# The down projection with every block sum on VectorE, its seven products in another order, and the last six k pairs summed token tile by token tile

## The chip, the cores and the metric

The kernel runs on one core of a Trainium2 chip. The engines that matter here are TensorE (PE in the profile, its weight loads PEld), VectorE (DVE), ScalarE (ACT) and GpSimd (POOL); SyncE (SP) issues most DMAs. Each engine takes its instructions in the order in which they stand, so an instruction that waits holds back all behind it. The metric is the device time of one execution in microseconds (us), median over the runs.

## The reference, cut to what matters

One decoder layer on 1024 tokens of width 1024: a token mixer, a cross-attention and a gated MLP, each between two RMSNorms. The change touches the last product of the MLP and the last norm with its residual:

```
u = causal_dwconv(h @ w_up, conv_w) + conv_b
a, b = split(u, 2)
y = (silu(a) * b) @ w_down            # (1024 x 2816) @ (2816 x 1024)
out = h2 + y * rsqrt(mean(y * y) + EPS) * g[5]
```

All of it is float32, with the accuracy of float32 products.

## The kernel before

**Where the stage lies.** The up projection runs column tile by column tile (Strassen's scheme, `strassen_pair`). Its last call ends with two short convolutions (`conv3`, L1127), a SiLU and a gate product (L1133) on VectorE and ScalarE; `silu(a) * b` goes to DRAM as `mid_d`, 22 rows of 128 channels x 1024 tokens. Then the down projection begins; TensorE passes from one to the other without a barrier.

**Strassen's scheme for the down projection.** The tokens are cut into two halves, the output columns into two halves, and the 22 k tiles into even and odd ones, which gives 11 k pairs (`kp`) and, for each pair, blocks A11 to A22 of the activations and B11 to B22 of the weights, all 128x512. `PRODS` lists the seven products M1 to M7; each is a sum of one or two A blocks times a sum of one or two B blocks, added up in PSUM over the 11 pairs. A product takes four PSUM banks, one for each tile of 128 tokens.

**A step** is one k pair of one product, so there are 7 x 11 = 77. `down_operands` makes its operands: it loads the blocks (an A block once, `a_block`; the B blocks each time into `rb`), sums them, and splits each sum into a high part, rounded to the matmul format (ScalarE, L132 or L1312 or L1308), and a low part, what the rounding lost (VectorE, L133 or L1313 or L1309). `mm3` then issues high x high, high x low and low x high (L236, L237, L238) for each of the four token tiles: twelve matmuls of 512 columns a step. Operands are made four steps ahead (`fetch(4)`, the tag `w` has four buffers).

**Who sums.** M4 and M3 have a sum of B blocks: GpSimd (L1301). M5 and M2 have a sum of A blocks: GpSimd (L1299). M1, M6 and M7 have both: A on GpSimd (L1299), B on VectorE (L1301). M2's B block is negated in its split.

**After a product** `done` adds its banks into the accumulators `yacc` (ScalarE copies for M4 and M3, VectorE adds, L1322, for the rest). When a half row of `yacc` is complete, `square` (ScalarE, L1318) sums its squares and `gained` multiplies it by the norm's gain (VectorE, L1326). `final` works out the norm's factor (L1338, L213 to L217), applies it with the residual `fin` (VectorE, L1332, two halves) and stores. `fin` has two buffers; `residual` (L1343) loads one. M6 and M7 add onto the banks of M2 and M1. The last four k pairs of M7 are walked token tile by token tile, so that the tiles end one after another; the residual of a tile is asked for just before its matmuls.

A scheduler sorts the instructions of each engine; the order inside one engine is not quite that of the code.

Of the kernel before, what the change touches and what calls it, by code (L numbers as in the profile page):

```python
# [1475 lines left out]
```

## Time and profile before

| | us |
|---|---|
| median of 3 runs (1509.54 to 1512.87) | 1512.68 |
| the profiled execution | 1516.54 |
| its span, first to last instruction | 1514.5 |
| TensorE busy in the span | 1445.2 (95%) |
| VectorE busy | 1179.0 (78%) |
| ScalarE busy | 698.9 (46%) |
| GpSimd busy | 301.2 (20%) |

The first matmul of the down projection starts at 1263.0 us of the span, the last at 1496.8. A busy share is a mean over the whole program; what holds in this stage is read from rows of this stage. Times in rows are us from the start of the span; the profile calls every product bank `M`, every operand `wM`, every block sum `sM`, every A block `ma`, every loaded B pair `rbM`.

### The profile page before, as it was taken

How to read it: one execution, taken by the hardware profiler on the slowest of the kernel's cores; microseconds unless marked ns; L12 is line 12 of the kernel's file. 1: busy time of each engine (PE TensorE's matmuls, PEld its weight loads, DVE VectorE, ACT ScalarE, POOL GpSimd, SP SyncE). 2: the span in 40 equal slices, each digit the busy share in tenths (PEclk: the TensorE clock that was granted, in tenths of full speed). 3: DMA queues.
4: the chain of work that ended last, by engine and by line, in shares of the span. 5: the costliest groups of instructions: out<-in, count | busy, mean ns of one | idle time of the engine just before them, and what ended most of it. 6: DMA issues, size and time to landing. Idle time of an engine off the chain costs nothing.

```text
span 1514.5 us, 19535 instructions
## 1 busy us (share of the span) xinstructions
PE 1445.2 (95%) x7099; PEld 1189.5 (79%) x7099; DVE 1179.0 (78%) x1938; ACT 698.9 (46%) x1348; POOL 301.2 (20%) x195
## 2 busy tenths in 40 slices
PE   6999999999999899999999979999999999999984
PEld 6878888888897778788888858888888887887763
DVE  6799999983577777734555877888888888869996
ACT  6527455533565445433433534444444444554342
POOL 0000000000000000000001543333333334655651
PEclk9999999999999999999999989999999999999997
DMA  7523133339656765401423112222222227964545
GB/s 250 173 75 124 44 112 84 112 111 327 185 160 211 241 209 179 149 1 42 154 85 110 43 56 84 78 76 84 84 84 84 84 84 260 317 201 161 184 160 176
DMA packets 118560, 205.74 MB, mean 136 GB/s; under 512 B 17184, under 2 KB 58816, under 8 KB 118464
## 3 DMA queue, kind: packets, MB, share of 16 engines
q1 hardware_dynamic: 95488, 155.99, 33.2%
q10 hardware_dynamic: 22976, 48.51, 8.6%
q8 instruction: 56, 0.92, 0.3%
q14 instruction: 40, 0.33, 0.1%
HBM read 153.58 MB, written 50.87 MB: 135 GB/s over the span
## 4 chain that ended last, share of the span: by engine, by line
PE 70%; DVE 13%; DMA 8%; issue 4%; ACT 3%; POOL 1%; SPq 0%; DVEq 0%; ACTq 0%; POOLq 0%
PE st L236 8%; PE st L238 8%; PE st L237 8%; PE pj L238 6%; PE pj L236 6%; PE pj L237 6%; DVE wM L133 3%; PE M L237 2%; PE M L236 2%; PE M L238 2%; PE y L237 2%; PE y L238 2%; PE y L236 2%; PE sc L237 1%; PE sc L236 1%
## 5 line engine op out<-in xcount | busy, mean ns | idle before, releaser
L352 DVE SCALAR_TENSOR_TENSOR ca<-sg,par,ca 128x1023 f32<-128x1023 f32 (+18 forms) x120 | 150.3, 1268 | 1.1
L236 PE MATMUL pj<-xT,w_in 128*128 128x512 f32 x384 | 150.8, 393 | 0.1
L238 PE MATMUL pj<-xT,w_in 128*128 128x512 f32 x384 | 150.3, 391 | 0.5 <-DVE w_in L133 0.5
L237 PE MATMUL pj<-xT,w_in 128*128 128x512 f32 x384 | 149.9, 390 | 0.0
L1198 POOL TENSOR_TENSOR xr<-x,x 128x256 f32<-128x256 f32 x32 | 32.4, 1045 | 582.6 <-DVE hr L1106 565.4
L237 PE MATMUL M<-wM 128*128 128x512 f32 x308 | 124.9, 406 | 9.8 <-DVE wM L133 5.7
L1127 DVE SCALAR_TENSOR_TENSOR ua<-ua,par 128x1023 f32<-128x1023 f32 x88 | 117.0, 1329 | 11.3 <-ACT ua L1125 8.4
L236 PE MATMUL M<-wM 128*128 128x512 f32 x308 | 120.8, 397 | 2.2 <-ACT wM L132 2.2
L238 PE MATMUL M<-wM 128*128 128x512 f32 x308 | 121.6, 395 | 0.0
L236 PE MATMUL st<-xT,wst 128*128 128x512 f32 x304 | 118.7, 391 | 0.0
L238 PE MATMUL st<-xT,wst 128*128 128x512 f32 x304 | 118.4, 390 | 0.0
L237 PE MATMUL st<-xT,wst 128*128 128x512 f32 x304 | 118.2, 389 | 0.0
L1299 POOL TENSOR_TENSOR sM<-ma,ma 128x512 f32<-128x512 f32 x55 | 95.1, 1732 | 73.5 <-DVE wM L133 45.0
L236 PE MATMUL st<-x,wst 128*128 128x512 f32 x228 | 93.3, 409 | 9.6 <-ACT ua L1216 5.7
L238 PE MATMUL st<-x,wst 128*128 128x512 f32 x228 | 91.0, 399 | 0.0
L237 PE MATMUL st<-x,wst 128*128 128x512 f32 x228 | 90.9, 399 | 0.0
L1157 DVE TENSOR_TENSOR wst<-sums,wst 128x512 fp32r<-128x512 f32 x76 | 60.7, 819 | 35.0 <-ACT wst L1156 35.0
L1156 ACT ACTIVATE wst<-sums 128x512 fp32r<-128x512 f32 x76 | 43.8, 621 | 90.0 <-POOL sums L1151 90.0
L237 PEld LDWEIGHTS M<-wM 128*128 128x128 f32 x308 | 58.9, 191 | 33.0 <-DVE wM L133 15.3
L238 PEld LDWEIGHTS pj<-xT,w_in 128*128 128x128 f32 x384 | 72.1, 188 | 15.4 <-DVE w_in L133 0.8
L236 PEld LDWEIGHTS pj<-xT,w_in 128*128 128x128 f32 x384 | 72.0, 188 | 14.9 <-ACT w_in L132 0.3
L237 PEld LDWEIGHTS pj<-xT,w_in 128*128 128x128 f32 x384 | 72.2, 188 | 14.5
(380 smaller groups left out, 3782.6 us busy)
## 6 DMA issues: line engine op xcount, KB each, us to landing
rbM<-in_w_down SPq DMA_DIRECT2D x132, 256.0 KB, 3.5
raw_up<-in_w_up SPq DMA_DIRECT2D x44, 512.0 KB, 3.6
raw_in<-in_w_in SPq DMA_DIRECT2D x24, 512.0 KB, 3.7
mid_d<-ua ACTq DMA_DIRECT2D x22, 512.0 KB, 2.6
ma<-mid_d SPq DMA_DIRECT2D x44, 256.0 KB, 5.0
raw_kv<-in_w_kv SPq DMA_DIRECT2D x16, 512.0 KB, 4.2
h_d<-h ACTq DMA_DIRECT2D x16, 512.0 KB, 2.7
xr<-in_x ACTq DMA_DIRECT2D x8, 512.0 KB, 5.3
```

The lines of the kernel that those rows point to most:

```text
L133: dve.tensor_tensor(w[:, 1], raw, w[:, 0], op=ALU.subtract)
L236: pe.matmul(o, lhsT=wh, rhs=xh, start=start, stop=False, skip_group_check=onto)
L237: pe.matmul(o, lhsT=wh, rhs=xl, start=False, stop=False, skip_group_check=onto)
L238: pe.matmul(o, lhsT=wl, rhs=xh, start=False, stop=stop, skip_group_check=onto)
L352: dve.scalar_tensor_tensor(out=ca[:, d:], in0=sg[:, :T - d], scalar=par[:, wb + 30 - d:wb + 31 - d], in1=ca[:, d:], op0=ALU.mult, op1=ALU.add)
L1127: dve.scalar_tensor_tensor(out=a[:, d:], in0=u[:, :T - d], scalar=fw(2 - d), in1=a[:, d:], op0=ALU.mult, op1=ALU.add)
L1156: act.activation(w[:, i, 0], op[s], AF.Copy)
L1157: dve.tensor_tensor(w[:, i, 1], op[s], w[:, i, 0], op=ALU.subtract)
L1198: nc.gpsimd.tensor_tensor(raw[n], X[n][0][:, :, s], X[n][1][:, :, s], op=ALU.add)
L1299: nc.gpsimd.tensor_tensor(sums[:, 0], A_s[0], A_s[1], op=alu(ab[2]))
```

## The change

In the down projection GpSimd computes nothing any more. Sums of B blocks (L1305) and of A blocks (L1312) are done by VectorE in place, in the tile `rb` itself, so the tag `sum` goes. Signs are placed otherwise, so that every A sum is a difference and M2 needs no negation. The B tiles have six buffers in place of four (`raw` 2, `braw` 4). The A21 blocks lie in three tiles of four.

The products run M4, M3, M2, M1, M6, M5, M7 (before: M4, M3, M5, M2, M1, M6, M7). M5 now starts on the banks that M6 has just ended. `gained` moves from `done` to the list `pend`, which is now worked off at odd k pairs of every product.

The last six k pairs of M7 (before: four) are walked token tile by token tile. Three of them (5, 6, 7) have operands in the A21 tiles, free by then, and are made among the last steps of M5. All four residuals are asked for before that walk; two of them lie in `raw` tiles.

```diff
-    LAST = 4
+    LAST = 6
+    PRODS = (("M4", 0, ("22",), ("21", "11")), ("M3", 1, ("11",), ("12", "22")),
+             ("M2", 0, ("22", "21"), ("11",)), ("M1", 1, ("11", "22"), ("11", "22")),
+             ("M6", 0, ("21", "11"), ("11", "12")), ("M5", 0, ("11", "12"), ("22",)),
+             ("M7", 1, ("12", "22"), ("21", "22")))
+    ENDP = len(PRODS) - 1
+    EXTRA = (5, 6, 7)
...
-        name, ab, bb = PRODS[m]
-        p, tag = ((wpool, "raw"), (dr, "braw"))[n_step[0] % 2]
+        name, _, ab, bb = PRODS[m]
+        p, tag, bufs = (wpool, "raw", 2) if n_step[0] % 3 == 0 else (dr, "braw", 4)
...
-        w = wpool.tile([P, 2, 2, 512], F32R, tag="w", name=f"w{name}_{kp}", bufs=4)
-        if len(ab) == 3 or len(bb) == 3:
-            sums = dr.tile([P, 2, 512], F32, tag="sum", name=f"s{name}_{kp}", bufs=2)
-        if len(ab) == 3:
-            nc.gpsimd.tensor_tensor(sums[:, 0], A_s[0], A_s[1], op=alu(ab[2]))
-        if len(bb) == 3:
-            (dve if len(ab) == 3 else nc.gpsimd).tensor_tensor(sums[:, 1], rb[:, 0], rb[:, 1], op=alu(bb[2]))
...
+        sync.dma_start(out=rb[:, 1], in_=at(bb[0]))
+        if len(bb) == 2:
+            sync.dma_start(out=rb[:, 0], in_=at(bb[1]))
+            dve.tensor_tensor(rb[:, 1], rb[:, 1], rb[:, 0], op=ALU.subtract if name == "M1" else ALU.add)
+        if m == ENDP and kp in EXTRA:
+            w = dl.tile([P, 2, 2, 512], F32R, tag="a21", name=f"w{name}_{kp}", bufs=3)
         else:
+            w = wpool.tile([P, 2, 2, 512], F32R, tag="w", name=f"w{name}_{kp}", bufs=4)
+        if len(ab) == 2:
+            dve.tensor_tensor(rb[:, 0], A_s[0], A_s[1], op=ALU.subtract)
+            split(w, rb)
+        else:
+            for i, r in enumerate((A_s[0], rb[:, 1])):
+                act.activation(w[:, 0, i], r, AF.Copy)
+                dve.tensor_tensor(w[:, 1, i], r, w[:, 0, i], op=ALU.subtract)
...
+        fin = raw_tile((P, D), f"fin{t}") if last else dl.tile([P, D], F32, tag="fin", name=f"fin{t}", bufs=2)
...
-            gained(hi, 1)
-            pend.append(lambda: final(hi, residual(hi), 0))
+            pend.append(lambda: (gained(hi, 1), final(hi, residual(hi), 0)))
+        elif name == "M5":
+            add_to(lo, 0, o)
+            add_to(lo, 1, o, -1)
+            square(lo, 1)
+            pend.append(lambda: gained(lo, 1))
...
+    todo = [(m, kp) for m in range(ENDP) for kp in range(NP)]
+    for n, kp in enumerate(EXTRA):
+        todo.insert(len(todo) - 3 + n, (ENDP, kp))
+    todo += [(ENDP, kp) for kp in range(NP) if kp not in EXTRA]
...
-            if pend and name == "M7" and kp % 2:
+            if pend and kp % 2 and kp < NP - 1:
...
-    fetch(LAST)
+    fetch()
+    fins.update({q: residual(q, q > 1) for q in range(4)})
     for q in range(4):
-        fins[q] = residual(q)
         for kp in range(NP - LAST, NP):
```

The order of the instructions shows three places. The first is VectorE at the start of the stage, where `ua` belongs to the last column tile of the up projection and `M4_2` is the third step of M4. Before:

```order
L1184 TENSOR_TENSOR ua43_10582<-st21_3_10586,p21_10587 128x512
L1127 SCALAR_TENSOR_TENSOR ua21_10581<-ua21_10581,par_78 128x1022
L1313 TENSOR_TENSOR wM4_1_10730<-sM4_1_10731,wM4_1_10730 128x512
L1313 TENSOR_TENSOR wM4_2_10742<-ma22_2_10737,wM4_2_10742 128x512
L1127 SCALAR_TENSOR_TENSOR ua43_10582<-ua43_10582,par_78 128x1023
L1313 TENSOR_TENSOR wM4_2_10742<-sM4_2_10743,wM4_2_10742 128x512
L1127 SCALAR_TENSOR_TENSOR ua43_10582<-ua43_10582,par_78 128x1022
L1313 TENSOR_TENSOR wM4_3_10754<-ma22_3_10749,wM4_3_10754 128x512
L1133 TENSOR_TENSOR ua21_10581<-ua21_10581,ua43_10582 128x1024
```

and now:

```order
L1184 TENSOR_TENSOR ua43_10582<-st21_3_10586,p21_10587 128x512
L1127 SCALAR_TENSOR_TENSOR ua21_10581<-ua21_10581,par_78 128x1023
L1317 TENSOR_TENSOR wM4_1_10730<-rbM4_1_10726,wM4_1_10730 128x512
L1127 SCALAR_TENSOR_TENSOR ua21_10581<-ua21_10581,par_78 128x1022
L1127 SCALAR_TENSOR_TENSOR ua43_10582<-ua43_10582,par_78 128x1023
L1305 TENSOR_TENSOR rbM4_2_10737<-rbM4_2_10737 128x512
L1127 SCALAR_TENSOR_TENSOR ua43_10582<-ua43_10582,par_78 128x1022
L1317 TENSOR_TENSOR wM4_2_10741<-ma22_2_10735,wM4_2_10741 128x512
L1133 TENSOR_TENSOR ua21_10581<-ua21_10581,ua43_10582 128x1024
L1317 TENSOR_TENSOR wM4_2_10741<-rbM4_2_10737,wM4_2_10741 128x512
```

The two convolutions (L1127) and the gate product (L1133) stand among the splits as before; now the B sum (L1305) of step 2 stands there too, and the second split of step 2 comes behind L1133.

The second place is VectorE where the last full product ends and M7's steps begin. Before, M6's banks (named M2, onto which M6 adds) are added (L1322) and multiplied by the gain (L1326) among M7's splits:

```order
L133 TENSOR_TENSOR wM6_10_12227<-sM6_10_12228,wM6_10_12227 128x1024
L1301 TENSOR_TENSOR sM7_1_12270<-rbM7_1_12266 128x512
L133 TENSOR_TENSOR wM7_0_12248<-sM7_0_12249,wM7_0_12248 128x1024
L1301 TENSOR_TENSOR sM7_2_12291<-rbM7_2_12287 128x512
L133 TENSOR_TENSOR wM7_1_12269<-sM7_1_12270,wM7_1_12269 128x1024
L1301 TENSOR_TENSOR sM7_3_12328<-rbM7_3_12324 128x512
L1322 TENSOR_TENSOR yacc4_10704<-yacc4_10704,M2_0_11571 128x512
L133 TENSOR_TENSOR wM7_2_12290<-sM7_2_12291,wM7_2_12290 128x1024
L1326 TENSOR_TENSOR yacc4_10704<-yacc4_10704,gb5_10698 128x512
L1322 TENSOR_TENSOR yacc5_10705<-yacc5_10705,M2_1_11572 128x512
L1322 TENSOR_TENSOR yacc6_10706<-yacc6_10706,M2_2_11573 128x512
L1322 TENSOR_TENSOR yacc7_10707<-yacc7_10707,M2_3_11574 128x512
```

Now it is M5's banks that are added (L1326, eight of them), between the splits of M7's steps 0 to 2 and those of 3 and 4:

```order
L133 TENSOR_TENSOR wM7_1_12235<-rbM7_1_12231,wM7_1_12235 128x1024
L133 TENSOR_TENSOR wM7_2_12255<-rbM7_2_12251,wM7_2_12255 128x1024
L1326 TENSOR_TENSOR yacc0_10700<-yacc0_10700,M5_0_11955 128x512
L1326 TENSOR_TENSOR yacc1_10701<-yacc1_10701,M5_1_11956 128x512 x2
L1326 TENSOR_TENSOR yacc2_10702<-yacc2_10702,M5_2_11957 128x512 x2
L1326 TENSOR_TENSOR yacc3_10703<-yacc3_10703,M5_3_11958 128x512 x2
L1305 TENSOR_TENSOR rbM7_3_12287<-rbM7_3_12287 128x512
L1305 TENSOR_TENSOR rbM7_4_12307<-rbM7_4_12307 128x512
L1312 TENSOR_TENSOR rbM7_3_12287<-ma12_3_11959,ma22_3_10746 128x512
L1312 TENSOR_TENSOR rbM7_4_12307<-ma12_4_11979,ma22_4_10769 128x512
L1330 TENSOR_TENSOR yacc0_10700<-yacc0_10700,gb5_10698 128x512
L133 TENSOR_TENSOR wM7_3_12291<-rbM7_3_12287,wM7_3_12291 128x1024
```

Where one sum on VectorE and one split made a step, two sums and one split do now, and the adds stand ahead of the sums of steps 3 and 4.

The third place is the end of SyncE's queue, with the residual loads (from `h2_d`) and the stores of the first halves (to `out`). Before, tiles 0 to 3:

```order
L1334 DMA out_0<-fin6_12482 128x512
L1343 DMA fin0_12544<-h2_d_70 128x1024
L1334 DMA out_0<-fin7_12519 128x512
L1343 DMA fin1_12576<-h2_d_70 128x1024
L1334 DMA out_0<-fin0_12544 128x512
L1334 DMA out_0<-fin1_12576 128x512
L1343 DMA fin2_12608<-h2_d_70 128x1024
L1343 DMA fin3_12640<-h2_d_70 128x1024
L1334 DMA out_0<-fin2_12608 128x512
L1334 DMA out_0<-fin3_12640 128x512
```

and now:

```order
L1347 DMA fin1_12393<-h2_d_70 128x1024
L1302 DMA rbM7_10_12369<-in_w_down 128x512
L1304 DMA rbM7_10_12369<-in_w_down 128x512
L1347 DMA raw_fin2_12395<-h2_d_70 128x1024
L1347 DMA raw_fin3_12397<-h2_d_70 128x1024
L1338 DMA out_0<-fin0_12391 128x512
L1338 DMA out_0<-fin1_12393 128x512
L1338 DMA out_0<-raw_fin2_12395 128x512
L1338 DMA out_0<-raw_fin3_12397 128x512
```

All four loads stand ahead of the four stores (that of tile 0 further up, ahead of M7's weights for pair 8); before, the loads of tiles 2 and 3 stood behind the stores of tiles 0 and 1.

## Rows read from the trace of the kernel before

**Rows 1.** The page's first line.
```profile
span 1514.5 us, 19535 instructions
```

**Rows 2.** Stretches: PE, PEld, DVE, ACT, POOL busy (instructions); granted clock; DMA share; GB/s.
```profile
1260.00:1280.00 20.00, 16.84 (x71) 12.44 (x70) 18.13 (x18) 10.16 (x15) 11.44 (x6) 1.00 0.87 303
1280.00:1360.00 80.00, 80.00 (x355) 66.24 (x354) 62.28 (x67) 44.19 (x81) 50.16 (x32) 1.00 0.82 273
1385.00:1460.00 75.00, 74.22 (x307) 55.98 (x307) 74.34 (x63) 28.72 (x34) 43.97 (x25) 1.00 0.55 179
1460.00:1490.00 30.00, 22.72 (x76) 16.38 (x75) 29.86 (x49) 11.65 (x18) 12.16 (x7) 0.84 0.43 148
1474.00:1477.00 3.00, 3.00 (x9) 2.32 (x8) 3.00 (x4) 0.91 (x1) 3.00 (x2) 0.50 0.34 109
1484.00:1490.00 6.00, 5.49 (x13) 4.19 (x14) 5.96 (x12) 1.52 (x2) 0.41 (x1) 0.50 0.41 141
```

**Rows 3.** Waits of 1385 to 1460: who for whom, total us, times, longest.
```profile
PEld M L237 <- DVE wM L133: 7.8, 19, 0.8
```

**Rows 4.** Timeline of one M6 step, VectorE and GpSimd: start us, duration us, instruction.
```profile
1432.54 0.69 DVE L1301 TENSOR_TENSOR sM<-rbM 128x512 f32<-128x512 f32 x1
1432.58 1.80 POOL L1299 TENSOR_TENSOR sM<-ma,ma 128x512 f32<-128x512 f32 x1 [1.76 <-DVE wM L133]
1433.15 2.32 DVE L133 TENSOR_TENSOR wM<-sM,wM 128x1024 fp32r<-128x1024 f32 x1
1435.50 0.69 DVE L1301 TENSOR_TENSOR sM<-rbM 128x512 f32<-128x512 f32 x1
```

**Rows 5.** Timeline of VectorE while GpSimd computes nothing.
```profile
1461.47 1.89 DVE L1326 TENSOR_TENSOR yacc<-yacc,gb 128x512 f32<-128x512 f32 x3
1463.27 1.22 DVE L133 TENSOR_TENSOR wM<-sM,wM 128x1024 fp32r<-128x1024 f32 x1
1464.41 0.68 DVE L1301 TENSOR_TENSOR sM<-rbM 128x512 f32<-128x512 f32 x1
1497.46 1.40 DVE L1332 SCALAR_TENSOR_TENSOR fin<-yacc,r_y,fin 128x512 f32<-128x512 f32 x2
```

**Rows 6.** Timeline of TensorE: first and last matmul of the stage.
```profile
1263.02 0.39 PE L236 MATMUL M<-wM 128*128 128x512 f32 x1
1496.84 0.39 PE L238 MATMUL M<-wM 128*128 128x512 f32 x1
```

**Rows 7.** Timeline of VectorE at the start of the stage.
```profile
1252.43 0.68 DVE L1176 TENSOR_TENSOR u<-st,p 128x512 f32<-128x512 f32 x1
1262.57 1.28 DVE L1127 SCALAR_TENSOR_TENSOR ua<-ua,par 128x1023 f32<-128x1023 f32 x1 [0.18 <-ACT ua L1125]
1263.77 0.68 DVE L1184 TENSOR_TENSOR ua<-st,p 128x512 f32<-128x512 f32 x1
```

**Rows 8.** Timeline of the end: one token tile's chain, and the last two halves.
```profile
1492.54 0.39 PE L238 MATMUL M<-wM 128*128 128x512 f32 x1
1492.96 1.28 DVE L1322 TENSOR_TENSOR yacc<-yacc,M 128x512 f32<-128x512 f32 x2 [2.57 <-PE M L238]
1493.69 0.63 ACT L1318 ACTIVATE sqj<-yacc 128x512 f32<-128x512 f32 x1 [4.77 <-DVE yacc L1322]
1494.22 0.19 ACT L1318 ACTIVATION_READ_ACCUMULATOR sqj<-yacc 128x1 f32 x1
1501.89 0.15 DVE L1338 TENSOR_TENSOR s<-ss 128x1 f32<-128x1 f32 x1
1502.86 0.16 DVE L217 SCALAR_TENSOR_TENSOR r_y<-r_u,r_y 128x1 f32<-128x1 f32 x1
1509.96 1.41 DVE L1332 SCALAR_TENSOR_TENSOR fin<-yacc,r_y,fin 128x512 f32<-128x512 f32 x2 [3.40 <-DMA fin<-h_d]
```

**Rows 9.** SyncE's own waits of 1460 to 1515, and DMA issues (KB, us to landing).
```profile
SPq L1343 <- DMA out<-fin: 16.5, 5, 4.4
fin<-h_d SPq DMA_DIRECT2D x8, 512.0 KB, 4.0
```

More of the change, by code (lines that the diff above doesn't have):

```diff
@@ L1275, in a_block @@
         if (b, kp) not in res:
-            res[b, kp] = (dr if b == "22" and kp < 8 else dl).tile([P, 512], F32, name=f"ma{b}_{kp}")
-            sync.dma_start(out=res[b, kp], in_=mid_d[2 * kp + int(b[1]) - 1][:, HS[int(b[0]) - 1]])
+            if b == "21":
+                if kp % 4 == 0:
+                    g = dl.tile([P, 4, 512], F32, tag="a21", name=f"ma21_{kp}", bufs=3)
+                    for i in range(4):
+                        res[b, "t", kp + i] = g[:, i]
+                t = res[b, "t", kp]
+            else:
+                t = (dr if b == "22" and kp < 8 else dl).tile([P, 512], F32, name=f"ma{b}_{kp}")
+            res[b, kp] = t
+            sync.dma_start(out=t, in_=mid_d[2 * kp + int(b[1]) - 1][:, HS[int(b[0]) - 1]])
         return res[b, kp]
@@ L1282, in down_operands @@
     def down_operands(m, kp):
-        name, ab, bb = PRODS[m]
-        p, tag = ((wpool, "raw"), (dr, "braw"))[n_step[0] % 2]
+        name, _, ab, bb = PRODS[m]
+        p, tag, bufs = (wpool, "raw", 2) if n_step[0] % 3 == 0 else (dr, "braw", 4)
         n_step[0] += 1
-        A_s = [a_block(b, kp) for b in ab[:2]]
-        rb = p.tile([P, 2, 512], F32, tag=tag, name=f"rb{name}_{kp}", bufs=2)
+        A_s = [a_block(b, kp) for b in ab]
+        rb = p.tile([P, 2, 512], F32, tag=tag, name=f"rb{name}_{kp}", bufs=bufs)
@@ L1339, in ss5_sum, with residual @@
         return s1
-    def residual(t):
-        fin = dl.tile([P, D], F32, tag="fin", name=f"fin{t}", bufs=2)
+    def residual(t, last=False):
+        fin = raw_tile((P, D), f"fin{t}") if last else dl.tile([P, D], F32, tag="fin", name=f"fin{t}", bufs=2)
         sync.dma_start(out=fin, in_=h2_d[t])
@@ L1354, in done @@
             act.activation(yacc[hi][:, HS[1]], o, AF.Copy)
-        elif name == "M5":
-            add_to(lo, 0, o, -1)
-            add_to(lo, 1, o)
-            square(lo, 1)
-            gained(lo, 1)
         elif name == "M2":
@@ L1362, in done @@
             square(hi, 0)
-            gained(hi, 0)
+            pend.append(lambda: gained(hi, 0))
         elif name == "M1":
@@ L1377, in hybrid_layer, with fetch @@
     fins = {}
-    todo = [(m, kp) for m in range(len(PRODS)) for kp in range(NP)]
+    todo = [(m, kp) for m in range(ENDP) for kp in range(NP)]
+    for n, kp in enumerate(EXTRA):
+        todo.insert(len(todo) - 3 + n, (ENDP, kp))
+    todo += [(ENDP, kp) for kp in range(NP) if kp not in EXTRA]
     dops = {}
-    def fetch(n):
-        while todo and len(dops) < n:
+    def fetch():
+        extra = lambda s: s[0] == ENDP and s[1] in EXTRA
+        while todo and (extra(todo[0]) or sum(not extra(s) for s in dops) < 4):
             s = todo.pop(0)
@@ L1390, in hybrid_layer @@
     banks = [None, None]
-    for m, (name, _, _) in enumerate(PRODS):
+    for m, (name, bset, _, _) in enumerate(PRODS):
         onto = name in ("M6", "M7")
         if not onto:
-            banks[m % 2] = [psum("b", f"{name}_{q}") for q in range(4)]
-        o = banks[m % 2]
-        early = NP - LAST if name == "M7" else NP
+            banks[bset] = [psum("b", f"{name}_{q}") for q in range(4)]
+        o = banks[bset]
+        early = NP - LAST if m == ENDP else NP
         for kp in range(early):
-            fetch(4)
+            fetch()
             w = dops.pop((m, kp))
```

25 lines of the change are left out of this document (4 added, 21 removed).

## The prediction, made before the change was run

> **What bounds the kernel now.** The order of reading was: the page, the stretches of the last 260 us, the waits in them, the timelines of the engines that wait, and the end.
>
> The page gives the span, 1514.5 us [rows 1]. The stretches show TensorE's need. From 1280 to 1360, in M4, M3 and M5, TensorE is busy all the time with 355 matmuls in 80 us [rows 2], less about two counted in both neighbours: 0.227 us from one start to the next, 2.72 us for the twelve of a step. The stage has 7 x 11 x 12 = 924, so 923 intervals or 209.5 us from its first start to its last at that pace. The trace has them at 1263.02 and 1496.84 [rows 6], 233.8 us apart. So 24.3 us are lost, and behind the last start come another 1514.5 - 1496.84 = 17.7 us.
>
> Where they are lost: in 1260 to 1280 there are 71 matmuls where 90 would fit (20 / 0.227 and two), 4.3 us. From 1385 to 1460, M1 and M6, there are 307 where 332 would fit, 5.7 us; VectorE is busy 74.34 of 75 us there, and TensorE waits for its split 19 times [rows 3]. From 1460 to 1490, M7, there are 76 where 134 would fit, 13.2 us, with VectorE again full (29.86 of 30). The rest, about 1 us, lies between.
>
> What makes VectorE full is seen in one M6 step [rows 4]. The split L133 starts while GpSimd's sum runs and takes 2.32 us; beside no GpSimd work it takes 1.22 [rows 5]. From one B sum to the next are 1435.50 - 1432.54 = 2.96 us, more than TensorE's 2.72. VectorE thus waits for the very sums that GpSimd takes off its hands.
>
> **The change part by part.**
>
> *Sums move to VectorE.* It gains 55 A sums and 22 B sums and loses the lock. Of an A sum on VectorE there is no row; the nearest is a B sum of the same shape, 0.68 us alone, and three like operations in a line take 1.89, so 0.60 from start to start [rows 5]. Between these ends I take 0.60, since most neighbours in the new order don't read each other. A split of 1024 columns takes 1463.27 to 1464.41, so 1.14 to the next start [rows 5]. A step then needs 0.60 + 2 x 0.60 = 1.80 us in M4 and M3, 0.60 + 1.14 = 1.74 in M2 and M5, 2 x 0.60 + 1.14 = 2.34 in M1, M6 and M7, all under 2.72. M1's 11 steps with M2's four adds and four gains are 25.7 + 4.8 = 30.5 us against TensorE's 29.9, which the four operand buffers (10.9 us ahead) cover. So the 5.7 us of M1 and M6 go, but for 0.3 that I keep for M5's start, whose banks are only free when the adds of M6 are done.
>
> The Trainium skill (Trace Analysis, Optimizing Scalar/DVE Operations) advises the opposite move when VectorE is saturated, work off to ScalarE or even GpSimd, and adds that for GpSimd it might not help, because of a shared read port. Rows 4 agree with the second half. By the first half alone VectorE would get worse; that is the fourth rival.
>
> *The start.* The last convolutions hold VectorE here. L1184 starts when the up projection's last matmul has ended, near 1263.4 (it was 1263.77 behind L1127 [rows 7]). Behind it stand, in the new order: 0.60; L1127 at 1.2 (1.28 [rows 7] less the overlap); the last split of step 1 at 0.6, so near 1265.8, when TensorE needs it; three more L1127 at 1.2, the B sum 0.6, a split 0.6, L1133 at 1.14 and only then the split that step 2 needs, 0.6. That ends 6.5 us later, at 1272.4; TensorE has done step 1 by 1268.5. The loss is 3.9, beside 4.3 before: no gain. Below, if loads come sooner than the order fears, it could be 2; above, since VectorE now stands in line for the B loads that GpSimd waited for, each late load adds itself; I allow 8. Steps 3 on are made at 1.80 a step, so it doesn't grow.
>
> SyncE takes one new wait: the loads of pair 6 stand ahead of the first A block and wait for the split of pair 0. On VectorE that stands right behind L1176 (1252.43 [rows 7]) and ahead of L1178, for which the next load in the queue waits in both kernels. So it hides under that wait; without that cover, its price would be the split's 0.68.
>
> *M5 and M7.* Here VectorE's new work piles up. From the first add of M6's banks to the split of M7's pair 10 its order holds 12 adds, 8 gains and 25 sums (45 at 0.60 = 27.0), 20 splits (22.8), 8 halves of `final` at 0.67, by 1.40 for two [rows 5] (5.4), and some 20 operations on single columns at about 0.1 (2.0): 57.2 us. They begin 1.6 us before M6 ends, and the last split waits another 0.9 for ScalarE's high part: pair 10 is ready 56.5 us after M6's end. TensorE would want it after eleven steps of M5 (29.9), five of M7 (13.6) and five pairs of the first token tile (3.4): at 46.9. So M7 comes 9.6 us late, first at its pair 0 and then behind the eight adds at pair 3. Before, M7 lost 13.2. If the 45 small ones need 0.68 each, it is 13.2 as before; if the waits are spread so that the three early operands hide them, 4.
>
> *The clock.* After M7's waits TensorE ran at 0.50 of its clock (1.2 GHz), from 1474 to 1477 and from 1484 to 1490 [rows 2]: 9 us, at the cost of some 4.5. Fewer waits, but two long ones, remain. I take 2 us; 0 to 4.5. The Trainium skill (TensorE: Matmul & The Clock Gate, Part 1) has the half clock as the default state, which activity lifts; by it the one long wait at the start could cost a stretch like that of 1474 too, 1.5 us more in the sum. In 1260 to 1280 the row shows 1.00 through shorter waits [rows 2]; no row here shows one of 3.9.
>
> *Six pairs by tiles and four early residuals.* Six pairs put the tiles' ends 6 x 3 x 0.227 = 4.1 us apart (before 2.7), more than the 3 us that VectorE needs for one. And the tail loses its loads: before, SyncE's residual loads waited 16.5 us in all for stores that had to leave the two buffers, and a load takes 4.0 [rows 9]; VectorE waited 3.40 for the last [rows 8]. With four buffers the third and fourth load wait only for M7's own splits, some 13 us before the end. The chain behind the last matmul is then, from rows 8: to the add 0.42; add to square 0.73; square and accumulator 0.72 (1493.69 to 1494.41); factor 1.13 (1501.89 to 1503.02); two halves 1.41; last store to the end of the span 1514.5 - 1511.37 = 3.13: 7.5 us in place of 17.7, a gain of 10.2. The gain's multiplication hides under the square. If the loads were late after all, the tail would keep one load and wait, 4.0 + 3.4.
>
> **Sum.** Lost: 3.9 + 0.3 + 9.6 + 2.0 = 15.8, before 24.3: 8.5 gained. With the tail's 10.2 that is 18.7 us, a span of 1495.8. The profiled execution took 1516.54 us, 2.0 more than its span and 3.9 more than the median of the runs; on the median of 1512.68 the forecast is 1494.0 us. From the term's bounds (start 2 to 8, M7 4 to 13.2, clock 0 to 4.5, tail 7.5 to 14.9), not all at one end at once, its own range is 1487 to 1501.
>
> **Rivals.**
>
> 1. *TensorE bounds it to the end.* The operands made early and those in the A21 tiles carry M7 through: losses 3.9 + 0.3 + 2 and no slow clock, 6.2, so 18.1 gained and 10.2 more: 1484.4. For it: VectorE's mean need over the products is under TensorE's. Against: the 57.2 us stand in one stretch of 46.9.
>
> 2. *The matmuls gain nothing, only the tail does.* M7's waits are as long as before and the clock falls, the start is worse by what M1 and M6 win: 24.3 lost as before, 1512.68 - 10.2 = 1502.5. For it: VectorE stays full from M5 on. Against: 5.7 us in M1 and M6 were the lock's.
>
> 3. *The change doesn't do what it says: the tail keeps its loads.* The two `raw` tiles come free too late, or stores hold them: tail 14.9, 1494.0 + 7.4 = 1501.4. Against: the `raw` tiles are read for the last time by the split of M7's pair 9.
>
> 4. *Slower: VectorE is slow for another reason than GpSimd.* If a split takes 2.32 us whatever GpSimd does (rows 4 and 5 differ by something else, such as the DMAs), two sums and a split are 3.52, over TensorE's 2.72; it decides from a split of 1.52 on. M1 and M6 then lose 22 x 0.80 = 17.6, and the stretch of 57.2 grows by 20 x 1.18 = 23.6: 15.8 + 41.2 - 24.3 = 32.7 worse, less the tail's 10.2: 1535. For it: the change asks more of the engine that is full. Against: the short split and the long one differ by the GpSimd sum beside them.
>
> **How the numbers follow.** Forecast 0.54, rival 1 0.18, rival 2 0.15, rival 3 0.08, rival 4 0.05. What a measurement here can tell from no change is about 0.3%, 4.5 us. Forecast and rivals 1 to 3 lie 10 us and more below; I take 0.05 off them for starts or loads worse than allowed, which end near no change. So faster 0.90, same 0.04, slower 0.06. The range of 8 in 10 takes in rival 1, 2 and 3: 1483 to 1505.
>
> **What would show it.** Right: no GpSimd row after the up projection; L133 at 1.22 in every step; TensorE without gaps in M1 and M6; waits of TensorE for VectorE at M7's pairs 0, 3 and 10, some 10 us in all; 7 to 8 us from the last matmul to the end, with no wait for `fin`. Wrong: gaps in M1 or M6, splits of 2.3 without GpSimd, a first step of M4 that waits for loads, or a last chain that waits for a residual.

## The result, and the profile after

The median of four executions is 1496.4 us (1494.95 to 1499.21) against 1512.8 before: a ratio of 0.989, 95% interval 0.987 to 0.991. Measured once more on another chip the ratio was 0.989 (0.987 to 0.991). So the change made the kernel faster by 1.1%, as forecast (1494.0, range 1483 to 1505).

The profiled execution took 1496.32 us, span 1494.5; that of before took 1516.54, 3.8 us above the median of 1512.8. The page's first lines, with busy time, share and instructions of each engine:

```profile
span 1494.5 us, 19452 instructions
PE 1434.6 (96%) x7099; PEld 1186.8 (79%) x7099; DVE 1161.3 (78%) x1993; ACT 695.3 (47%) x1326; POOL 169.5 (11%) x118
```

VectorE (DVE) executes 55 instructions more than the 1938 of before and is busy for 17.7 us less (1179.0 before). GpSimd's 77 sums are gone (195 instructions before).

The split at L133, with the least, median and largest duration in ns; in the kernel before, 16 of its 33 took 1.7 to 2.3 us beside a GpSimd sum [rows 4]:

```profile
L133 DVE TENSOR_TENSOR wM<-rbM,wM x55: 1206/1224/1249, 1319.9 to 1471.2; 128x1024 fp32r<-128x1024 f32 x55
```

The down projection by stretches, the operands' instructions only (TensorE, its loads, VectorE, ScalarE busy, each with its instructions; clock; DMA share; GB/s), which answers to [rows 2]:

```profile
1255.00:1280.00 25.00, 14.51 (x58) 10.68 (x59) 8.90 (x14) 8.40 (x15) 1.00 0.90 310
1280.00:1360.00 80.00, 80.00 (x354) 66.25 (x353) 36.53 (x45) 32.26 (x44) 1.00 0.86 298
1360.00:1440.00 80.00, 80.00 (x354) 66.09 (x353) 37.36 (x31) 32.66 (x31) 1.00 0.55 176
1440.00:1472.00 32.00, 26.66 (x107) 20.50 (x106) 11.54 (x10) 9.43 (x10) 0.95 0.65 215
```

From 1280 to 1440 TensorE has no gap: M1 and M6 lie in there, which lost 5.7 us before [rows 2, 3]. From 1440 to 1472, around M7's start, 141 matmuls would fit and 107 are there: 34 x 0.227 = 7.7 us lost. The first stretch holds 58 matmuls from the first start at 1261.96 on, where 80 would fit: 22 x 0.227 = 5.0 us lost.

M7's two waits on TensorE's timeline (start, duration, in brackets the idle time before and what ended it), and the last matmul:

```profile
1449.19 0.50 PE L237 MATMUL M<-wM 128*128 128x512 f32 x1 [1.58 <-DVE wM L133]
1460.50 0.97 PE L236 MATMUL M<-wM 128*128 128x512 f32 x3 [3.46 <-ACT wM L132]
1484.32 0.39 PE L238 MATMUL M<-wM 128*128 128x512 f32 x1
```

The end, answering to [rows 8]: VectorE's add of tile 2, tile 2's last halves, tile 3's add, square and gain, and tile 3's halves.

```profile
1480.93 0.68 DVE L1326 TENSOR_TENSOR yacc<-yacc,M 128x512 f32<-128x512 f32 x1
1484.81 1.41 DVE L1336 SCALAR_TENSOR_TENSOR raw_fin<-yacc,r_y,raw_fin 128x512 f32<-128x512 f32 x2
1486.14 0.68 DVE L1326 TENSOR_TENSOR yacc<-yacc,M 128x512 f32<-128x512 f32 x1
1486.92 0.63 ACT L1322 ACTIVATE sqj<-yacc 128x512 f32<-128x512 f32 x1 [2.78 <-DVE yacc L1326]
1487.67 0.69 DVE L1330 TENSOR_TENSOR yacc<-yacc,gb 128x512 f32<-128x512 f32 x1 [0.85 <-ACT sqj L1322]
1489.44 1.41 DVE L1336 SCALAR_TENSOR_TENSOR raw_fin<-yacc,r_y,raw_fin 128x512 f32<-128x512 f32 x2
```

No wait for a residual is left (3.40 us before [rows 8]). But the last add starts 1.82 us after the last matmul's start, because the halves of tile 2 stand ahead of it, and the gain (L1330) stands between square and factor.

**How kernels are compared below.** The up projection, which no kernel here changes, started its last matmul between 1255.7 and 1264.3 us in the profiled executions. So the times are compared by their ratio to runs of before on the same chip (medians 1512.6 to 1515.2 there), and a trace is read from the first matmul of the down projection on: what its 924 matmuls lose against 209.5 us, and what comes behind the last start. Of after: 1484.32 - 1261.96 = 222.4, so 12.9 lost, and 10.2 behind.

| kernel | median us | ratio to before, 95% | lost | behind | sum |
|---|---|---|---|---|---|
| before | 1512.8 | | 24.3 | 17.7 | 42.0 |
| after | 1496.4 | 0.989 (0.987 to 0.991) | 12.9 | 10.2 | 23.1 |
| after, other chip | 1495.4 | 0.989 (0.987 to 0.991) | 13.1 | 10.1 | 23.2 |
| before + sums on VectorE | 1497.7 | 0.990 (0.989 to 0.992) | 5.9 | 19.0 | 24.9 |
| before + residuals early | 1506.7 | 0.996 (0.995 to 0.997) | 22.9 | 12.2 | 35.1 |
| before + both | 1492.2 | 0.985 (0.982 to 0.987) | 6.8 | 15.1 | 21.9 |
| both, factor ahead of gain | 1494.0 | 0.986 (0.983 to 0.988) | 7.0 | 16.8 | 23.8 |
| after, A sums on GpSimd | 1506.6 | 0.995 (0.994 to 0.997) | 26.6 | 9.7 | 36.3 |
| after + idle GpSimd sums | 1526.0 | 1.009 (1.007 to 1.010) | 42.9 | 10.0 | 52.9 |
| after, last four pairs | 1490.0 | 0.983 (0.981 to 0.986) | 9.1 | 12.6 | 21.7 |
| after, factor ahead of gain | 1495.3 | 0.986 (0.984 to 0.988) | 13.2 | 9.6 | 22.8 |
| after, no upper finals | 1487.3 | 0.983 (0.981 to 0.985) | 5.2 | 9.2 | 14.4 |
| both + hoisted difference | 1492.4 | 0.987 (0.985 to 0.989) | 4.7 | 16.5 | 21.2 |
| the same, residuals in weight buffers | 1491.3 | 0.986 (0.984 to 0.988) | 3.2 | 16.6 | 19.8 |

### The profile page after: what moved, and what is told of

The parts are those of the page before. It is cut to its first block, busy times and chain, and to the rows that moved or that the text cites. A ratio compares the mean times of both kernels' runs of the same rounds, so it can differ in the third digit from the quotient of the medians.

```text
span 1494.5 us, 19452 instructions
## 1 busy us (share of the span) xinstructions
PE 1434.6 (96%) x7099; PEld 1186.8 (79%) x7099; DVE 1161.3 (78%) x1993; ACT 695.3 (47%) x1326; POOL 169.5 (11%) x118
## 4 chain that ended last, share of the span: by engine, by line
PE 49%; DVE 6%; DMA 3%; issue 2%; ACT 2%; POOL 1%; DVEq 0%; SPq 0%; ACTq 0%; POOLq 0%
PE st L236 8%; PE st L238 8%; PE st L237 8%; PE M L237 3%; PE M L238 3%; PE M L236 3%; PE y L237 2%; PE y L238 2%; PE y L236 2%; PE sc L236 1%; PE sc L237 1%; PE sc L238 1%; PE wo L237 1%; PE wo L238 1%; PE wo L236 1%
## 5 line engine op out<-in xcount | busy, mean ns | idle before, releaser
L237 PE MATMUL M<-wM 128*128 128x512 f32 x308 | 121.1, 393 | 4.6 <-DVE wM L1317 2.7
L1127 DVE SCALAR_TENSOR_TENSOR ua<-ua,par 128x1023 f32<-128x1023 f32 x88 | 115.6, 1315 | 9.7 <-ACT ua L1125 7.0
L236 PE MATMUL M<-wM 128*128 128x512 f32 x308 | 118.9, 392 | 4.4 <-ACT wM L132 3.5
L238 PE MATMUL M<-wM 128*128 128x512 f32 x308 | 120.8, 392 | 0.0
L132 ACT ACTIVATE wM<-rbM 128x1024 fp32r<-128x1024 f32 x55 | 58.0, 1062 | 75.1 <-PE M L238 53.7
L133 DVE TENSOR_TENSOR wM<-rbM,wM 128x1024 fp32r<-128x1024 f32 x55 | 67.0, 1226 | 8.4 <-ACT wM L132 8.4
```

What stands on the lines that cost most here:

```text
L132: act.activation(w[:, 0], raw, AF.Copy)
L133: dve.tensor_tensor(w[:, 1], raw, w[:, 0], op=ALU.subtract)
L236: pe.matmul(o, lhsT=wh, rhs=xh, start=start, stop=False, skip_group_check=onto)
L237: pe.matmul(o, lhsT=wh, rhs=xl, start=False, stop=False, skip_group_check=onto)
L238: pe.matmul(o, lhsT=wl, rhs=xh, start=False, stop=stop, skip_group_check=onto)
L1127: dve.scalar_tensor_tensor(out=a[:, d:], in0=u[:, :T - d], scalar=fw(2 - d), in1=a[:, d:], op0=ALU.mult, op1=ALU.add)
```

## The experiments

**1. The sums alone.** The kernel before, with the sums' engine changed and nothing else.

```diff
-            nc.gpsimd.tensor_tensor(sums[:, 0], A_s[0], A_s[1], op=alu(ab[2]))
+            dve.tensor_tensor(sums[:, 0], A_s[0], A_s[1], op=alu(ab[2]))
-            (dve if len(ab) == 3 else nc.gpsimd).tensor_tensor(sums[:, 1], ...
+            dve.tensor_tensor(sums[:, 1], ...
```

> The kernel before with one edit: the sums of blocks that GpSimd computed are on VectorE (order of products, last four pairs, tail all as before). By the prediction's own terms: the splits of M1, M6 and M7 at L133 fall from 2.32 to about 1.22 us, the 5.7 us that M1 and M6 lose go, M7's loss goes from 13.2 to about 9.6, the 17.7 us of the tail stay: 9.3 us less than before, about 1503. Rival A (a split takes 2.3 us beside any work of that kind, whoever sums): the step of M1 and M6 costs VectorE 0.6 + 0.6 + 2.3 = 3.5 us against TensorE's 2.72, 22 steps x 0.8 = 17 us more than before, about 1530. Rival B (the sums' place is worth nothing, all the gain is tail and reordering): 1511 to 1514.

Measured: 1497.7 us, 15.7 less than before and 6 better than expected. Rivals A and B fall. The page's line of the engines, the split, and the stretches of M1, M6 and M7:

```profile
PE 1433.4 (96%) x7099; PEld 1188.0 (79%) x7099; DVE 1163.3 (78%) x2015; ACT 698.4 (47%) x1348; POOL 169.9 (11%) x118
L133 DVE TENSOR_TENSOR wM<-sM,wM x33: 1215/1224/1227, 1377.8 to 1473.1; 128x1024 fp32r<-128x1024 f32 x33
1360.00:1440.00 80.00, 80.00 (x355) 66.24 (x354) 38.41 (x39) 32.77 (x37) 1.00 0.59 191
1440.00:1472.00 32.00, 31.47 (x138) 25.35 (x137) 10.96 (x9) 8.99 (x10) 1.00 0.53 174
```

VectorE took on 77 instructions (1938 to 2015) and its busy time fell by 1179.0 - 1163.3 = 15.7 us. At 0.60 us each, the pace from one start to the next [rows 5], the 77 are 46 us, so GpSimd had cost VectorE 46 + 15.7 = 62 us for them: 0.80 us a sum, more than VectorE needs to do it itself. And M7, which I expected to lose 9.6 us still, loses 0.7 to 1472 (138 matmuls of 141) and 1.8 to its end. So the order of before, with the sums moved, is hardly late in M7.

**2. The residuals alone.** The kernel before, four buffers asked for ahead of the last walk.

```diff
-        fin = dl.tile([P, D], F32, tag="fin", name=f"fin{t}", bufs=2)
+        fin = raw_tile((P, D), f"fin{t}") if last else dl.tile([P, D], F32, tag="fin", name=f"fin{t}", bufs=2)
...
+    fins.update({q: residual(q, q > 1) for q in range(4)})
     for q in range(4):
-        fins[q] = residual(q)
```

> The kernel before with one edit: the residual rows of the last four token tiles are asked for together, ahead of the tile by tile walk, into four buffers. By the prediction's tail term (17.7 to 7.5): 10.2 us less than before, about 1502.5. By the reading of the trace of after (a tile's chain on VectorE takes 4.6 to 5 us, not 3, the gain is not hidden, tail 10.2): 7.5 us less, about 1505. If SP's wait for fin is not what the end stood on: no change, 1512.

Measured: 1506.7, 6.8 less; in the trace the tail falls from 17.7 to 12.2. That is near the reading of after's trace (7.5); the prediction's term (10.2), which was for the residuals and the six pairs together, is not reached. The rows show VectorE's end: add of the first two tiles, then the halves of the four, with no wait for a load.

```profile
1487.18 1.29 DVE L1322 TENSOR_TENSOR yacc<-yacc,M 128x512 f32<-128x512 f32 x2 [1.07 <-PE M L238]
1491.68 1.40 DVE L1332 SCALAR_TENSOR_TENSOR fin<-yacc,r_y,fin 128x512 f32<-128x512 f32 x2
1494.34 1.42 DVE L1332 SCALAR_TENSOR_TENSOR fin<-yacc,r_y,fin 128x512 f32<-128x512 f32 x2 [0.33 <-DVE r_a L214]
1496.77 1.42 DVE L1332 SCALAR_TENSOR_TENSOR raw_fin<-yacc,r_y,raw_fin 128x512 f32<-128x512 f32 x2
1498.74 1.42 DVE L1332 SCALAR_TENSOR_TENSOR raw_fin<-yacc,r_y,raw_fin 128x512 f32<-128x512 f32 x2
```

From the first add at 1487.18 to the end of the last half at 1500.2 are 13.0 us for four tiles, 3.2 each, while TensorE delivers a tile every 2.7: with the loads gone, VectorE's own work is the tail.

**3. The A sums back on GpSimd.** The kernel after, 33 sums undone.

```diff
-            dve.tensor_tensor(rb[:, 0], A_s[0], A_s[1], op=ALU.subtract)
+            (nc.gpsimd if len(bb) == 2 else dve).tensor_tensor(rb[:, 0], ...
```

> The kernel after with one edit undone: the difference of the token operand's blocks in M1, M6 and M7 is computed on GpSimd again (33 sums). By the theory that GpSimd's two-input sum and VectorE's hold each other up: L133 back to 2.3 us, the 5.7 us of M1 and M6 back, M7's loss from 8.2 to about 13, in all 8 to 12 us more than after, 1504 to 1508. By the rival that the order of products and the four braw buffers gave the gain: within 2 us of after, 1494 to 1498, since VectorE is relieved of 33 x 0.6 = 20 us.

Measured: 1506.6, 10 to 11 more than after. VectorE has 33 instructions less than after (1960) and is busy for longer (1170.1 us against 1161.3); six of the 55 splits take up to 2.3 us again, and from 1360 to 1440, in M1, M6 and the start of M5, the gaps are back (317 matmuls of 354, 8.4 us).

```profile
L133 DVE TENSOR_TENSOR wM<-rbM,wM x55: 1199/1214/2315, 1317.5 to 1482.1; 128x1024 fp32r<-128x1024 f32 x55
1360.00:1440.00 80.00, 74.41 (x317) 57.94 (x316) 36.68 (x28) 30.29 (x29) 1.00 0.48 157
```

By the count of run 1, 33 sums on GpSimd cost VectorE 8.8 + 33 x 0.60 = 28.6 us, 0.87 each. But here ScalarE also waits for GpSimd's results (24.6 us in all), so this run alone doesn't tell holding up from waiting.

**4. GpSimd sums that nobody needs.** The kernel after, with one subtraction more per step of M1, M6 and M7 on GpSimd, into a buffer that nobody reads.

```diff
+    scr = dl.tile([P, 512], F32, name="scr")
...
+            if len(bb) == 2:
+                nc.gpsimd.tensor_tensor(scr, rb[:, 0], w[:, 0, 0], op=ALU.subtract)
```

> The kernel after with one addition: in each step of M1, M6 and M7 GpSimd subtracts two blocks (128x512) into a buffer that nobody reads, started when the step's rounding on ScalarE is done, so beside the split on VectorE. No instruction of another engine waits for it, but for the reuse of the step's buffers. By the theory of holding each other up: L133 goes from 1.22 to 1.8 to 2.3 us, VectorE's step from 2.34 to about 3.2 us against TensorE's 2.72, some 0.5 us x 22 steps in M1 and M6 and 1.0 x 11 in M7, about 20 us more than after, 1510 to 1525. By the rival that only waiting for GpSimd's result cost time: 1496, L133 at 1.22.

Measured: 1526.0, 30 more than after, a little above the expected span of 1510 to 1525. Nobody waits for these results; only the reuse of a step's buffers waits for GpSimd, 4.9 us on ScalarE in three waits and 1.2 us on VectorE in one. The rise in VectorE's busy time holds none of these waits: it is the holding up alone. Page line and groups (total us, mean ns):

```profile
PE 1445.2 (95%) x7099; PEld 1191.0 (78%) x7099; DVE 1191.8 (78%) x1993; ACT 695.1 (46%) x1326; POOL 243.6 (16%) x151
L1316 POOL TENSOR_TENSOR scr<-rbM,wM 128x512 f32<-128x512 f32 x33 | 73.7, 2232 | 192.9 <-ACT wM L132 187.5 <-DVE yacc L1329 3.0 <-DVE yacc L1333 1.7
L133 DVE TENSOR_TENSOR wM<-rbM,wM 128x1024 fp32r<-128x1024 f32 x55 | 75.2, 1374 | 7.2 <-ACT wM L132 4.3 <-DMA fin<-h_d 2.9
L1313 DVE TENSOR_TENSOR rbM<-ma,ma 128x512 f32<-128x512 f32 x55 | 49.9, 922 | 1.9 <-POOL scr L1316 1.2 <-DMA ma<-mid_d 0.3
```

The same 1993 instructions of VectorE take 1191.8 - 1161.3 = 30.5 us more: 0.92 us for each GpSimd sum. The split pays less than expected: eight of 55 take over 2 us, the others 1.2 to 1.4, 8.2 us in all. The A sums pay 12.5 us (mean 0.92 us; 0.69 in after), the B sums 4.9.

The ends of these instructions show how they are held up. In the trace of before each of the 16 long splits ends 1.08 or 1.09 us after the GpSimd sum beside it ([rows 4]: 1435.47 and 1434.38), and each of the 39 VectorE instructions of 512 columns that took over 0.9 us ends 0.55 us after. In this run the eight and the 19 end by the same 1.08 and 0.55. These are nearly the 1.14 and 0.60 us that such instructions need in a line [rows 5], so one that meets a GpSimd sum does almost all its work after the sum's end. The adds that read a bank of PSUM are not held up: in before, 14 of them start during a GpSimd sum and none takes more than 0.68 us.

The Trainium skill (SBUF — State Buffer, Who interferes with whom) says that a VectorE instruction with two SBUF inputs contends with a GpSimd instruction that reads SBUF, and that such contention is an exclusive lock. These rows agree.

**5. The two that gain, together.** The order of before, the last four pairs of before, sums on VectorE (run 1) and residuals early (run 2).

> The kernel before with the two edits that gained alone: all sums on VectorE (15.7 us alone) and the four residual buffers asked for ahead of the walk (6.8 us alone); the order of products, the last four pairs and the buffers stay as before. If the reordering and the last six pairs of the kernel after cost what the sums' move would give (M7's 8.2 us lost in after, 0.5 in the run with the sums alone): 1513.5 - 15.7 - 6.8 = 1491, some 5 us less than after. If the two gains are the same microseconds (the end then stands on VectorE's last factors either way): no better than the sums alone, 1496 to 1498, the same as after.

Measured: 1492.2, ratio 0.985 (0.982 to 0.987). After's interval begins at 0.987; by the medians the difference is 3 to 4 us, by the ratios 7, where 5 were expected. The two gains of 15.7 and 6.8 add up to 22.5, and 23.0 were measured. So the sums and the residuals are the whole gain; the rest of the change (order, buffers, last six pairs) together brought nothing on top. In its trace M7 loses 0.9 us to 1472 (137 of 141 matmuls). VectorE is full there and up to its last halves, which end at 1487.00 (busy for 9.99 of 10 and 11.31 of 12 us):

```profile
1440.00:1472.00 32.00, 31.49 (x137) 25.16 (x136) 10.94 (x9) 9.53 (x9) 1.00 0.61 193
1460.00:1470.00 10.00, 9.49 (x41) 7.23 (x40) 9.99 (x24) 3.66 (x5) 0.00 (x0) 1.00 0.69 217
1475.00:1487.00 12.00, 0.40 (x2) 0.00 (x0) 11.31 (x35) 3.54 (x12) 0.00 (x0) 0.71 0.60 221
```

**6. The last four pairs again.** The kernel after with two numbers changed.

```diff
-    LAST = 6
+    LAST = 4
-    EXTRA = (5, 6, 7)
+    EXTRA = ()
```

> The kernel after with the walk of the last six pairs put back to the last four (the three extra operand buffers not used): order of products, sums and residuals as in after. With four pairs the last operands are wanted 2 x 2.72 - 1.36 = about 4 us later, so M7's loss of 8.2 should fall to about 4, while the walk leaves 2.7 us per tile and the tail grows from 10.2 to about 12.2 (as in the run of before with the residuals ahead): 2 us less than after, 1494.5. If the last six pairs are what kept the tail short and M7's loss is set by VectorE's work alone: 2 to 4 us more than after, 1499.

Measured: 1490.0, ratio 0.983 (0.981 to 0.986), the fastest kernel that computes the whole reference. Both halves of the expectation are in the trace: M7 loses 2.3 us (131 of 141) in place of 7.7, and the tail grows from 10.2 to 12.6: 3.0 us less, where 2 were expected. The medians lie 5 to 6 apart (after: 1496.4 and 1495.4). Of the rest some lies ahead of the stage, where nothing was changed (the up projection's last matmul started at 1255.9 us against 1258.8 and 1261.5). The start of the stage, also unchanged, gives 1.5 back, since the clock fell there (last row of this document); one profiled execution of each can't say more. Against run 5 (0.985), which has the order of before, the intervals overlap: the order with its buffers makes no difference that is shown. The last six pairs cost 5 to 6 us by the medians, 3.0 of them seen in M7 and the tail.

```profile
1440.00:1472.00 32.00, 30.60 (x131) 23.69 (x130) 13.18 (x11) 9.31 (x9) 1.00 0.51 166
```

**7 and 8. The factor ahead of the gain.** In the last four tiles `gained` is emitted behind the root, once in after and once in the kernel of run 5.

```diff
-    def final(t, fin, first):
+    def final(t, fin, first, then=lambda: None):
...
         r = sqrt_r(ss5_sum(t), 1, "r5")
+        then()
...
-            gained(lo, 0)
-            final(lo, fins.pop(lo), 1)
+            final(lo, fins.pop(lo), 1, lambda: gained(lo, 0))
```

> The kernel after with one edit: in the last four tiles the gain's multiplication (L1330, 0.69 us) is emitted behind the root instead of between square and sum. The prediction's tail had it hidden under the square; the trace of after shows it between square and sum in each tile, so that a tile's chain takes 4.6 to 5 us of VectorE against TensorE's 4.1. By that reading: 0.6 us less at the last tile and up to 1.4 more where the tiles queue, 0.6 to 2 us less than after, 1494.5 to 1496. If the tail's length is TensorE's walk and the store: no difference (under 0.5 us).

> The kernel before with all sums on VectorE, the residuals asked for ahead, and in the last four tiles the gain's multiplication of 0.69 us emitted behind the root instead of between square and sum. By the theory that the gain stands on the last chain (0.6 us at the last tile, more where a tile's chain waits for the one ahead): 0.5 to 2 us less than the same kernel without it, 1489 to 1490.5. If VectorE's sum of work in the tail is the bound and not the order: no difference (under 0.5 us).

Measured: in after 1495.3; its ratio of 0.986 (0.984 to 0.988) overlaps that of after, so no difference is shown in the time. In the trace the tail is 9.6, 0.6 less: the last tile's share. The queue of tiles stays: TensorE's last matmul starts at 1483.94 here, so by the 0.42 us of [rows 8] the last add could start at 1484.36 and is 1.3 late. The four adds of tiles 0 to 3:

```profile
1473.03 0.69 DVE L1326 TENSOR_TENSOR yacc<-yacc,M 128x512 f32<-128x512 f32 x1 [1.49 <-PE M L238]
1477.22 0.68 DVE L1326 TENSOR_TENSOR yacc<-yacc,M 128x512 f32<-128x512 f32 x1
1481.40 0.68 DVE L1326 TENSOR_TENSOR yacc<-yacc,M 128x512 f32<-128x512 f32 x1
1485.63 0.68 DVE L1326 TENSOR_TENSOR yacc<-yacc,M 128x512 f32<-128x512 f32 x1
```

They stand 4.2 us apart, with the wait for the square in each tile's chain, against TensorE's 4.1. In the kernel of run 5 there was no gain either (1494.0 against 1492.2, intervals overlapping); a wait for a residual took its place there (the profile names "issue", but the load of this residual landed at 1478.82):

```profile
1478.90 1.41 DVE L1333 SCALAR_TENSOR_TENSOR fin<-yacc,r_y,fin 128x512 f32<-128x512 f32 x2 [2.10 <-issue]
```

**9. Without the upper finals.** The kernel after, with that part of VectorE's work taken out of the stretch between M6 and M7.

```diff
-            pend.append(lambda: (gained(hi, 1), final(hi, residual(hi), 0)))
+            pend.append(lambda: gained(hi, 1))
```

> The kernel after with the factors and the output of the upper token half left out (so that half of the output is not written): 4 x (1.41 + 0.7) us, in all some 8 us of VectorE's work between M6 and the last operands of M7. By the theory that M7's loss of 8.2 us is VectorE's backlog: M7's loss falls to 1 to 2, 6 to 7 us less than after, 1489 to 1490. By the rival that the operands are late for another reason (ScalarE's rounding, which waits 53.7 us for buffers, or the loads): within 1.5 us of after, 1495 to 1498.

Measured: 1487.3, 8.2 less than after on the same chip. M7's loss is gone to the last matmul:

```profile
1440.00:1472.00 32.00, 32.00 (x141) 25.91 (x140) 12.14 (x10) 9.43 (x9) 1.00 0.38 122
```

So the loss of after in M7 is VectorE's backlog, not ScalarE's rounding (L132), although ScalarE is named as the releaser of the longest wait: it waits for VectorE's sums itself (17.3 us in seven waits, in after). Fewer loads go along with the finals (DMA share 0.38 against 0.65), but in after's trace TensorE, VectorE and ScalarE nowhere wait for a load from 1414 to 1473, so the loads are not what was late.

**10 and 11. A sum moved to where VectorE has time.** In the kernel of run 5, the difference of blocks 12 and 22, which M7 needs, is formed in place during M2.

```diff
-             ("M7", ("12", "22", -1), ("21", "22", 1)))
+             ("M7", ("12",), ("21", "22", 1)))
...
+        if name == "M2":
+            d = res["12", kp]
+            dve.tensor_tensor(d, d, res["22", kp], op=ALU.subtract)
```

> The order of products of before, all sums on VectorE, residuals ahead of the walk, and one edit more: the difference of the token blocks 12 and 22 that M7 needs is formed in place of block 12 during M2 (11 subtractions of 0.60 us), where VectorE's step is 1.8 of TensorE's 2.72 us and after which nothing else reads block 12. By the theory that from M6's end to the last store VectorE's sum of work is the bound, wherever the walk begins: 11 x 0.60 = 6.6 us leave that stretch, up to 6 us less than the same kernel without the edit (1492.2), 1486 to 1488. By the rival that the stretch is bound by TensorE and the residual loads: within 2 us of 1492.

> As the kernel with the difference formed ahead in M2, and the last four residuals all go into buffers of weights (two of wpool's, two of dr's) instead of two of them waiting for the buffers of the upper token half. The trace of the kernel without this shows a last wait of 2.3 us for the second tile's residual. By the theory that VectorE's work is the bound and a wait in it counts in full: 1 to 2.3 us less, 1484 to 1487. If the chain behind the last matmul is the bound: no difference.

Measured: 1492.4, no gain over 1492.2. The hoist itself works: M7 has no gap (141 of 141), and VectorE's last split starts 4.2 us earlier (1467.84, in run 5 at 1472.00) though its stage began 1.9 later. (Without a sum of A blocks M7's split is two instructions of 512 columns, not one of 1024.) Then VectorE stands still for the residual of the last tile of the upper half, with the adds of the lower tiles queued behind it:

```profile
1440.00:1472.00 32.00, 31.99 (x141) 26.04 (x140) 13.27 (x20) 11.52 (x20) 1.00 0.60 195
1467.84 0.68 DVE L1316 TENSOR_TENSOR wM<-sM,wM 128x512 fp32r<-128x512 f32 x1
1472.29 1.42 DVE L1335 SCALAR_TENSOR_TENSOR fin<-yacc,r_y,fin 128x512 f32<-128x512 f32 x2 [3.70 <-DMA fin<-h_d]
```

With the last four residuals in weight buffers (1491.3) the same wait is 4.5 us. The loads of the upper half still take turns in two buffers: this one is issued at 1463.52, after the store from its buffer landed at 1463.45. It landed 210.8 us after the stage's first matmul, and 211.5 in run 10:

```profile
1468.88 1.42 DVE L1335 SCALAR_TENSOR_TENSOR fin<-yacc,r_y,fin 128x512 f32<-128x512 f32 x2 [4.48 <-DMA fin<-h_d]
```

It has the least loss of the complete kernels in its trace (19.8), but its median is not told apart from run 5 or 6. An earlier load of the upper half's last residual is the next step; it was not tried.

**12. After once more**, on the chip of runs 9 to 11.

> The kernel after, unchanged, on the chip of the three others, so that they stand against it without the spread between chips: 0.989 of before, 1494 to 1498 us. If the 1496.4 measured first was a slow sample of its spread (the up projection's end alone lies between 1255.7 and 1261.9 us in the profiled runs so far): 1490 to 1493.

Measured: 1495.4, 0.989. The first value was no slow sample.

## Why the prediction was right, and where its steps were not

The time came within 2.4 us, by a right mechanism and by terms that missed in both directions. That they cancel is luck.

- *The lock goes.* Right. L133 is 1.22 us in all 55 steps, M1 and M6 are without a gap, and runs 1, 3 and 4 each give the price of a GpSimd sum to VectorE: 0.80, 0.87 and 0.92 us. Rival 4, a split that is long whatever GpSimd does, falls with run 1.
- *The start.* Forecast 3.9, measured 5.0, within its bounds of 2 to 8. The split of step 2, forecast to end at 1272.4, ends at 1273.0. VectorE waits for B loads, as feared (9.4 us in eight waits in the whole stage). The 0.3 for M5's start is not seen: 1280 to 1440 is full.
- *M7 late.* Forecast 9.6 and 2.0 for the clock, measured 7.7 with the clock (at 0.95 of full speed over those 32 us, 1.6 us of it). VectorE's stretch was sized well: from 1414.62 to 1472.44 it is busy for 57.20 of 57.82 us, against 57.2. Run 9 shows that this backlog is the cause. By the prediction's own reckoning pair 10 was 9.0 late (1472.44 against 1416.46, M6's end, and 46.9). Waits came at pairs 0 and 3; the third, at pair 10, did not. And the clock should not have been added to the lateness: where VectorE's last split sets the end, a slower TensorE ahead of it only waits less. In after once more the clock was low for twice as long (a mean of 0.57 over 8 us, over 4 in after), and the matmuls lost 13.1 in place of 12.9, by one trace each. The half clock that the prediction named as possible at the stage's start did not come in after. What the prediction did not ask is how much of the lateness the change itself brings in: with the last six pairs the last operands of M7 are wanted some 4 us sooner, and three are made ahead of those of pairs 0 to 4. Counted to 1472, the same order with four pairs loses 2.3 (run 6), and the order of before 0.7 (run 1). The sums had already removed the loss that I put down to M7's load on VectorE.
- *The tail* is the step whose mechanism failed. Forecast 7.5, measured 10.2. "More than the 3 us that VectorE needs for one" and "the gain's multiplication hides under the square" are wrong. The gain stands behind the square on the chain (0.6 us). VectorE ends tile 2's chain before it adds tile 3, and with the wait for the square in each chain it falls behind TensorE's 4.1 a tile: the adds of tiles 2 and 3 lie 5.2 us apart, and 4.2 with the gain moved (run 7), so tile 2 holds the last add up by 1.4 (1.3 in run 7). The last store takes 3.65 in place of 3.13 (0.5). The residuals' part was right: no wait for `fin`, as run 2 shows by itself.
- *The sum.* Lost among the matmuls 12.9 (forecast 15.8), tail 10.2 (7.5): 23.1 against 23.3. M7 with its clock was forecast 3.9 too high, the start 1.1 and the tail 2.7 too low. What the prediction did not weigh is that six pairs, against four (run 6), shorten the time behind the last matmul by 2.4 us and lose 5.4 ahead of it, because VectorE is full there.

Rival 1 (TensorE bounds it to the end, 1484.4) is not reached; nearest comes run 9 with VectorE's work taken out (1487.3). Rival 2's 1502.5 and rival 3's 1501.4 are excluded by the time and by the missing wait for `fin`.

What stays open are the 2 to 3 us by which the medians of after and run 6 differ beyond what M7 and the tail show.

## What to carry to other kernels

Work put on GpSimd beside VectorE is not free: here each 128x512 sum cost VectorE 0.8 to 0.9 us, more than the 0.60 for doing it itself; look for one line with two durations, and test with a sum that nobody reads. Where one engine is full almost to the end, an earlier deadline (the longer walk by tiles) moved the wait from behind the last matmul to ahead of it and lost more than it won. Less work on that engine shortened the time (run 9); the same work in an earlier, slack place did not, since a load decided next (run 10). Time each part of a change alone: two of the parts here gave 23 us together, and the six pairs took 5 to 6 us back.
